# A float32 layer pair: token tiles of both halves in turn ahead of each feed-forward, stores on the ACT queue, another buffer layout in the down phase

## The chip, the cores and the metric

One NeuronCore of a Trainium2 chip. The time is that of one execution in device microseconds, lower is better. Times are medians of several runs; the profile is one further execution.

## What is computed

Two transformer layers one after the other on one sequence of 1024 tokens of width 1024, in float32, with one output of the same shape. The first has a pooling and a differential attention mixer and a gated feed-forward, the second a gated linear attention and a sliding window mixer, cross attention and a convolutional feed-forward. Cut to what the change touches:

```python
# first layer
h = h + rms_norm(jnp.einsum('bsd,de->bse', m, w_out), mix_post_g)
u = rms_norm(h, ffn_pre_g)
f = jax.nn.silu(jnp.einsum('bsd,df->bsf', u, w_ffn_gate)) * jnp.einsum('bsd,df->bsf', u, w_ffn_up)
h = h + rms_norm(jnp.einsum('bsf,fd->bsd', f, w_ffn_down), ffn_post_g)
...
# second layer, last part
h = h + cross_attn(rms_norm_2(h, norm_cross[l]), ...)
h = h + conv_ffn(rms_norm_2(h, norm_ffn[l]), w_up[l], conv_w[l], conv_b[l], w_down[l])
return rms_norm_2(h, norm_final)

def conv_ffn(h, w_up, conv_w, conv_b, w_down):
    u = h @ w_up                       # 1024 x 5632
    u = ...                            # causal convolution of width 3 over the tokens, per channel
    gate, val = jnp.split(u, 2, axis=-1)
    return (jax.nn.silu(gate) * val) @ w_down
```

## The kernel before, in words

Every matmul is done in three: each operand x is split into a high part (`bh`, `wh`: an ACT cast) and a low part (`bl`, `wl`: a DVE subtraction, L54 and L55, function `split`), and hi*hi, lo*hi and hi*lo are summed in PSUM (L75 to L77, L687 to L689). The 1024 tokens are eight tiles of 128; tiles 0 to 3 are the first half and 4 to 7 the second. `big` holds the transposed activations of each half as `bh0/bl0` (`_64`, `_65` in the rows) and `bh1/bl1` (`_66`, `_67`).

**The projection ahead of a feed-forward** (`close_square`, called for `wo`, `wo2` and `woc`) goes through the token tiles in the order 0 to 7. For each tile it multiplies (`mm(i, 0)`, `mm(i, 1)`), and `core` adds the residual (tile `x`, one buffer) and stores the sum to DRAM (`h1d`, `h3d`, `h4d`). `norm_un` squares and sums it on ACT, takes the reciprocal root on POOL and scales it on DVE (L146). Two tiles later `next_T` transposes it on PE: `to_T` (L156) for a tile of the first half; `u_second` (L719) for one of the second half, if a feed-forward follows.

**The feed-forwards** (`ffn`) use a seven-product scheme over 2x2 blocks: token halves by halves of the inner width. `u_second` makes the left forms: a11 and a12 are the first half's blocks, a22, s1, s2, s3 and s4 combine both halves, so tile 4 needs tile 0, 5 needs 1, and so on. In the kernel before it first rebuilds the first half's values r11 and r12 as hi + lo on POOL (L713), and one subtraction (L728) and the split of s3 are POOL's too.

**The up phase** goes over 22 weight tiles: gate weight `wraw` (two raw buffers), up weight `ru` (one). `t_forms` makes the right forms with four POOL sums (L771 to L775), `early` multiplies a11 and a12 by the gate weight, `rest` the other five products; L804 and L805 add up v, then comes the activation. PE takes the early products of three tiles ahead, and the first three before the loop. After each even tile `down_t` makes the right forms of the down weights for that step k (four loads, four POOL adds L821, four stores to `td`); after each odd one `down_s` makes the left forms s1, s2, s4 and a difference on DVE and stores seven blocks to `sd`.

**The down phase** (`down7`) reads both back in blocks of 512 KB into eight raw buffers `r` (L890), splits each and multiplies; the order of products is a11, s1, s2, s4, s3, a22, with six blocks of plain weights (`ws`) before a22 and the eighth operand, a12, at the end. There are 78 such blocks. `final` then normalizes: after the first feed-forward `left` loads h1, stores h2 (`h2d`, L1046) and prepares the next mixer.

A scheduler of the framework sets the order on each engine from the program's order and its own costs. All transfers are issued on the SP queue, in order: one that waits holds all behind it.

## Time and profile before

| | |
|---|---|
| median of 3 runs | 2789.79 us (2788.11 to 2793.65) |
| the profiled execution | 2791.67 us, span 2790.1 us, mean granted clock 0.984 |
| PE / DVE / ACT / POOL busy | 2679.0 / 1663.6 / 1143.4 / 609.7 us |
| first feed-forward, up phase | about 709 to 1167 us |
| first feed-forward, down phase | about 1167 to 1400 us |
| second feed-forward, up phase | about 2096 to 2570 us |
| second feed-forward, down phase | about 2571 us to the end |

PE is TensorE, DVE VectorE, ACT ScalarE, POOL GpSimd, SP the queue that issues transfers. "Idle" in brackets is the engine's idle time just before a group of instructions, with what ended it. Durations of single PE instructions overlap; their starts tell the pace.

### The profile page before, as it was taken

The page shows a single profiled execution, that of the slowest core. Times are in us where ns is not written, and L with a number is a line of the kernel's source. Part 1 is how long each engine was busy: PE and PEld are TensorE (multiplying, and loading weights), DVE is VectorE, ACT ScalarE, POOL GpSimd, SP SyncE. Part 2 cuts the span into 40 slices and gives each one's busy share as a digit, 9 for nine tenths or more (in the row PEclk, how much of TensorE's full clock was granted, in tenths as well). Part 3 has the DMA queues.
Part 4 walks back from the last instruction along what each step waited for, and adds up shares of the span by engine and source line. Part 5 has one row for each costly group of instructions (what it writes and reads, how often), then busy time and mean ns, then how long its engine had stood idle before and what let it go on. Part 6 is the DMA issues. An engine that isn't in the chain of part 4 may idle for free. (4 is left out here: it accounts for less than half of the span.)

```text
span 2790.1 us, 33443 instructions
## 1 busy us (share of the span) xinstructions
PE 2679.0 (96%) x12618; PEld 2179.0 (78%) x12618; DVE 1663.6 (60%) x2536; ACT 1143.4 (41%) x1950; POOL 609.7 (22%) x457
## 2 busy tenths in 40 slices
PE   8999999999699999999899999999997999999998
PEld 7776788888478888788788877888875777777887
DVE  6657415354665555446645557544547999997555
ACT  5555413133333333344443266342324444444443
POOL 1000000001655555000101000000017556652000
PEclk9999999999899999999999999999998999999999
DMA  3000111132344444486321102341223434444863
GB/s 132 31 16 12 53 46 42 56 124 91 106 172 145 148 162 151 176 269 226 123 81 38 57 20 94 133 129 31 70 91 108 159 133 150 155 152 153 295 230 128
DMA packets 145058, 327.04 MB, mean 117 GB/s; under 512 B 13168, under 2 KB 25856, under 8 KB 144896
## 3 DMA queue, kind: packets, MB, share of 16 engines
q1 hardware_dynamic: 144896, 324.91, 34.0%
q8 instruction: 99, 1.62, 0.2%
q14 instruction: 63, 0.52, 0.1%
HBM read 238.87 MB, written 85.98 MB: 116 GB/s over the span
## 5 line engine op out<-in xcount | busy, mean ns | idle before, releaser
L116 POOL TENSOR_TENSOR rstd<-ms,mhalf 128x1 f32<-128x1 f32 (+1 forms) x106 | 63.7, 604 | 1301.7 <-DVE ms L114 878.6
L55 DVE TENSOR_TENSOR wl<-wraw,wh 128x1024 fp32r<-128x1024 f32 (+2 forms) x161 | 201.0, 1253 | 219.9 <-ACT wh L54 215.4
L687 PE MATMUL single<-bh,wh 128*128 128x512 f32 x704 | 280.9, 404 | 42.4 <-ACT wh L54 26.5
L75 PE MATMUL gemm<-bh,wh 128*128 128x512 f32 x800 | 319.7, 400 | 0.0
L77 PE MATMUL gemm<-bh,wl 128*128 128x512 f32 x800 | 317.6, 397 | 0.7 <-DVE wl L55 0.7
L76 PE MATMUL gemm<-bl,wh 128*128 128x512 f32 x800 | 318.2, 398 | 0.0
L54 ACT CAST wh<-wraw 128x1024 fp32r<-128x1024 f32 (+2 forms) x161 | 160.9, 1002 | 302.8 <-PE gemm L76 161.9
L688 PE MATMUL single<-bl,wh 128*128 128x512 f32 x704 | 277.9, 395 | 2.7 <-DVE bl L55 2.7
L689 PE MATMUL single<-bh,wl 128*128 128x512 f32 x704 | 276.6, 393 | 0.0
L687 PEld LDWEIGHTS single<-bh,wh 128*128 128x128 f32 x704 | 134.6, 191 | 85.5 <-DVE v L805 31.4
L55 DVE TENSOR_TENSOR wl<-sum,wh 128x1024 fp32r<-128x1024 f32 x88 | 133.5, 1517 | 94.1 <-ACT wh L54 92.9
L54 ACT CAST wh<-sum 128x1024 fp32r<-128x1024 f32 x88 | 92.7, 1053 | 230.4 <-PE single L688 196.9
L821 POOL TENSOR_TENSOR tmp<-tmp 128x512 f32<-128x512 f32 x88 | 149.0, 1695 | 148.3 <-DMA tmp<-w2d 71.4
L75 PEld LDWEIGHTS gemm<-bh,wh 128*128 128x128 f32 x800 | 151.5, 189 | 33.3 <-issue 3.2
L77 PEld LDWEIGHTS gemm<-bh,wl 128*128 128x128 f32 x800 | 151.5, 189 | 32.7 <-DVE wl L55 1.1
L76 PEld LDWEIGHTS gemm<-bl,wh 128*128 128x128 f32 x800 | 151.5, 189 | 31.9 <-issue 1.1
L688 PEld LDWEIGHTS single<-bl,wh 128*128 128x128 f32 x704 | 134.5, 191 | 30.4 <-DVE bl L55 3.4
L689 PEld LDWEIGHTS single<-bh,wl 128*128 128x128 f32 x704 | 133.8, 190 | 29.5 <-DVE wl L55 0.6
L75 PE MATMUL gemm<-wh,bh 128*128 128x256 f32 (+2 forms) x448 | 151.8, 341 | 1.7 <-ACT wh L54 1.6
L77 PE MATMUL gemm<-wh,bl 128*128 128x256 f32 (+2 forms) x448 | 150.2, 336 | 0.0
L76 PE MATMUL gemm<-wl,bh 128*128 128x256 f32 (+2 forms) x448 | 149.6, 334 | 0.0
L55 DVE TENSOR_TENSOR bh<-r,bh 128x1024 fp32r<-128x1024 f32 x72 | 86.3, 1222 | 86.9 <-ACT bh L54 86.5
(406 smaller groups left out, 6510.7 us busy)
## 6 DMA issues: line engine op xcount, KB each, us to landing
r<-sd SPq DMA_DIRECT2D x60, 512.0 KB, 5.5
td<-tmp SPq DMA_DIRECT2D x88, 256.0 KB, 2.1
r<-td SPq DMA_DIRECT2D x40, 512.0 KB, 6.1
sd<-tmp SPq DMA_DIRECT2D x66, 256.0 KB, 2.3
wraw<-wg SPq DMA_DIRECT2D x22, 512.0 KB, 3.4
ru<-wu SPq DMA_DIRECT2D x22, 512.0 KB, 3.8
tmp<-wd SPq DMA_DIRECT2D x44, 256.0 KB, 3.8
sd<-v SPq DMA_DIRECT2D x44, 256.0 KB, 2.2
```

The source lines that it names most:

```text
L54: nc.scalar.copy(hi, src)
L55: (eng or nc.vector).tensor_tensor(out=lo, in0=src, in1=hi.bitcast(F32), op=ALU.subtract)
L75: nc.tensor.matmul(out, ah, bh, start=(i == 0), stop=False)
L76: nc.tensor.matmul(out, ah, bl, start=False, stop=False)
L77: nc.tensor.matmul(out, al, bh, start=False, stop=(i == n - 1))
L116: nc.gpsimd.tensor_tensor(out=r, in0=ms, in1=self.mhalf[:, 0:w], op=ALU.pow)
L687: nc.tensor.matmul(out, w[0], m[0], start=start, stop=False, skip_group_check=more)
L688: nc.tensor.matmul(out, w[0], m[1], start=False, stop=False, skip_group_check=more)
L689: nc.tensor.matmul(out, w[1], m[0], start=False, stop=stop, skip_group_check=more)
L821: nc.gpsimd.tensor_tensor(out=x, in0=x, in1=y, op=ALU.add)
```

## The change

- `close_square` goes through the tiles as 0, 4, 1, 5, 2, 6, 3, 7 where a feed-forward follows (`wo` and `woc`).
- The first half's transposes are copied once more by ACT (`keep`, tile `raw`), and `u_second` takes r11 and r12 from there. Its subtraction and the split of s3 go from POOL to DVE.
- `up_first` loads and splits three gate weights, the third through a buffer of another tag; `t_forms` loads that third weight a second time for its sums.
- The stores to h1d, h2d, h3d and h4d are issued on the ACT queue, behind the square that reads the same tile; so are the `sd` stores of the last step k.
- The right forms of both down weights are made in the first feed-forward's up phase, those of w2d after its odd tiles; the second one makes none.
- `down7` has two pools of four raw buffers, `ra` first in memory and `rb`. From block 49 on all blocks take `ra`, and `final` takes `rb`.

How the order of instructions changes, at three places. First PE where the first projection ends and the feed-forward begins: `un_6030`, `un_6140` and `un_6225` are tiles 5, 6 and 7 before; `un_6069`, `un_6159` and `un_6252` are tiles 6, 3 and 7 in the change. Before:

```order
L719 MATMUL single_6200<-ident_68,un_6030 128x128 x4
L719 MATMUL single_6205<-ident_68,un_6030 128x128 x4
L719 MATMUL single_6263<-ident_68,un_6140 128x128 x4
L719 MATMUL single_6268<-ident_68,un_6140 128x128 x4
L687 MATMUL single_6288<-bh0_64,wh_6165 128x512
L688 MATMUL single_6288<-bl0_65,wh_6165 128x512
```

In the change:

```order
L723 MATMUL single_6227<-ident_68,un_6069 128x128 x4
L723 MATMUL single_6232<-ident_68,un_6069 128x128 x4
L160 MATMUL single_6285<-ident_68,un_6159 128x128 x4
L160 MATMUL single_6293<-ident_68,un_6159 128x128 x4
L693 MATMUL single_6301<-bh0_64,wh_6184 128x512
L693 MATMUL single_6302<-bh0_64,wh_6184 128x512
```

The early products now stand behind tile 3's transposes, which they read. The hi*hi matmuls of four products go first.

DVE at the same place; `x_6226` (before) and `x_6253` (change) are tile 7's residual, `bl0` the low part of the first half, `bl1` that of the second. Before:

```order
L675 SCALAR_TENSOR_TENSOR un_6225<-single_6169,rstd1_6235,gain_5434 128x512
L677 TENSOR_TENSOR x_6226<-x_6226,un_6225 128x1024
L727 TENSOR_TENSOR t1_6260<-single_6268,r21_6259 128x512
L114 TENSOR_SCALAR ms1_6243<-ss1_6241 128x1
L146 SCALAR_TENSOR_TENSOR un_6225<-x_6226,rstd1_6245,gain_5436 128x1024
L729 SCALAR_TENSOR_TENSOR r11_6257<-t1_6260,r11_6257 128x512
L55 TENSOR_TENSOR bl1_67<-single_6268,bh1_66 128x4x128
L730 SCALAR_TENSOR_TENSOR r12_6258<-r12_6258,r11_6257 128x512
```

In the change:

```order
L732 TENSOR_TENSOR r21_6225<-raw_6142,r21_6225 128x512
L55 TENSOR_TENSOR bl1_67<-single_6232,bh1_66 128x4x128
L733 SCALAR_TENSOR_TENSOR raw_6142<-t1_6226,raw_6142 128x512
L55 TENSOR_TENSOR bl1_67<-t1_6226,bh1_66 128x4x128
L734 SCALAR_TENSOR_TENSOR raw_6142<-raw_6142 128x512
L55 TENSOR_TENSOR s2l_5847<-raw_6142,s2h_5846 128x4x128
L55 TENSOR_TENSOR s3l_5849<-r21_6225,s3h_5848 128x4x128
L55 TENSOR_TENSOR s4l_5851<-raw_6142,s4h_5850 128x4x128
L684 TENSOR_TENSOR x_6253<-x_6253,un_6252 128x1024
L55 TENSOR_TENSOR bl0_65<-single_6285,bh0_64 128x4x128
L55 TENSOR_TENSOR bl0_65<-single_6293,bh0_64 128x4x128
L114 TENSOR_SCALAR ms1_6270<-ss1_6267 128x1
```

Tile 7's residual add stands behind tile 6's forms, and the two splits of tile 3 (`bl0`) behind both.

ACT at the end of the first feed-forward's up phase; `g_9290` and `g_9449` are the last tile's gate, `r` the first blocks of the down phase. Before:

```order
L800 COPY v_9291<-single_9294 128x512
L801 COPY v_9291<-single_9264 128x512
L54 CAST bh0_64<-r_9408 128x1024
L1006 ACTIVATE g_9290<-single_9264 128x512
L54 CAST bh0_64<-r_9412 128x1024
L54 CAST bl0_65<-r_9416 128x1024
```

In the change:

```order
L54 CAST bh1_66<-r_9603 128x1024
L54 CAST bl1_67<-r_9635 128x1024
L1020 ACTIVATE g_9449<-single_9423 128x512
L820 DMA sd_81<-v_9450 128x512 x2
L820 DMA sd_81<-tmp_9524 128x512
L820 DMA sd_81<-tmp_9525 128x512
L820 DMA sd_81<-v_9310 128x512
L820 DMA sd_81<-tmp_9526 128x512
L54 CAST bh0_64<-r_9583 128x1024
L54 CAST bh0_64<-r_9587 128x1024
```

The last silu is followed by six stores, the last of them of `down_s`'s last form, and then by the casts of the first product's blocks.

The diff, cut to its core:

```diff
-    def norm_un(self, h, g, un):
+    def norm_un(self, h, g, un, dst=None):
         nc = self.nc
         ss = self.tiny(1, "ss")
         nc.scalar.activation(un, h, AF.Square, accum_out=ss)
+        if dst is not None:
+            nc.scalar.dma_start(out=dst, in_=h)
         r = self.rstd(ss, D)
         nc.vector.scalar_tensor_tensor(out=un, in0=h, scalar=r, in1=g, op0=ALU.mult, op1=ALU.mult)
 
-    def to_T(self, un, big, i, bank):
+    def to_T(self, un, big, i, bank, keep=False):
         nc = self.nc
         half, c = divmod(i, 4)
+        if keep:
+            self.raw = self.pus.tile([128, KT, 128], F32, tag="raw", name="raw")
         s = slice(c * 128, (c + 1) * 128)
         for k4 in range(2):
             ps = bank()
                 nc.tensor.transpose(ps[:, kt * 128:(kt + 1) * 128], un[:, x:x + 128], self.ident)
             self.split(big["h", half][:, k4 * 4:k4 * 4 + 4, s], big["l", half][:, k4 * 4:k4 * 4 + 4, s],
                        ps.rearrange("p (k t) -> p k t", k=4))
+            if keep:
+                nc.scalar.copy(self.raw[:, k4 * 4:k4 * 4 + 4, :], ps.rearrange("p (k t) -> p k t", k=4))

...
-            self.to_T(un, big, i, bank)
+            self.to_T(un, big, i, bank, self.second is not None)

...
-        self.td = tc.dram_tile([4, NK, 128, 512], F32, name="td")
+        self.td = {w: tc.dram_tile([4, NK, 128, 512], F32, name="td" + w) for w in ('wd', 'w2d')}

...
-            for i in range(2):
+            order = [0, 4, 1, 5, 2, 6, 3, 7] if self.second is not None else list(range(NT))
+            for i in order[:2]:
                 if (i, 0) not in pss:
                     mm(i, 0)
-            for i in range(NT):
+            for n, i in enumerate(order):
                 mm(i, 1)
-                if i >= 2:
+                if n >= 2:
                     self.next_T(self.single)
                 un = self.un()
-                h = core(p, i, (pss[i, 0], pss[i, 1]), un, gs)
-                self.norm_un(h, gs[-1], un)
+                h, dst = core(p, i, (pss[i, 0], pss[i, 1]), un, gs)
+                self.norm_un(h, gs[-1], un, dst)
                 self.pend.append((un, new, i))
-                if i + 2 < NT and (i + 2, 0) not in pss:
-                    mm(i + 2, 0)
-                if extra and extra.get(i):
-                    extra[i]()
+                if n + 2 < NT and (order[n + 2], 0) not in pss:
+                    mm(order[n + 2], 0)
+                if extra and extra.get(n):
+                    extra[n]()

...
-            nc.sync.dma_start(out=self.h1d[i], in_=x)
-            return x
+            return x, self.h1d[i]

...
-        r11, r12, r21, s1 = (self.pus.tile([128, 4, 128], F32, tag=n, name=n) for n in ("r11", "r12", "r21", "t1"))
-        for r, n in ((r11, "a11"), (r12, "a12")):
-            h, l = f[n]
-            nc.gpsimd.tensor_tensor(out=r, in0=h[:, :, s].bitcast(F32), in1=l[:, :, s].bitcast(F32), op=ALU.add)
+        r11, r12 = self.raw[:, 0:4, :], self.raw[:, 4:8, :]
+        r21, s1 = (self.pus.tile([128, 4, 128], F32, tag=n, name=n) for n in ("r21", "t1"))
...
         nc.vector.tensor_tensor(out=s1, in0=ps[1], in1=r21, op=ALU.subtract)
-        nc.gpsimd.tensor_tensor(out=r21, in0=r11, in1=r21, op=ALU.subtract)
+        nc.vector.tensor_tensor(out=r21, in0=r11, in1=r21, op=ALU.subtract)
         nc.vector.scalar_tensor_tensor(out=r11, in0=s1, scalar=-1.0, in1=r11, op0=ALU.mult, op1=ALU.subtract)
         nc.vector.scalar_tensor_tensor(out=r12, in0=r12, scalar=-1.0, in1=r11, op0=ALU.mult, op1=ALU.subtract)
         put("a22", ps[1])
         put("s1", s1)
         put("s2", r11)
         put("s4", r12)
-        put("s3", r21, nc.gpsimd)
+        put("s3", r21)
 
     def up_first(self, wg):
-        self.rg0 = self.up_rg(wg, 0)
+        self.rg0 = [self.up_rg(wg, 0), self.up_rg(wg, NK)]
+        x = self.pw.tile([128, 1024], F32, tag="wl", name="wr", bufs=self.nw)
+        self.nc.sync.dma_start(out=x, in_=self.d[wg][1])
+        self.rg0.append((None, self.up_pair(x)))

...
+                if rg is None:
+                    rg = self.pw.tile([128, 1024], F32, tag="wraw", name="wraw", bufs=self.nraw)
+                    nc.sync.dma_start(out=rg, in_=d[wg][t])
...
-                nc.sync.dma_start(out=self.sd[form, k], in_=x)
-
-            def down_t(k):
-                b = []
-
+                (nc.scalar if k == NK - 1 else nc.sync).dma_start(out=self.sd[form, k], in_=x)
+
+            def down_t(wd, k):
...
-                    nc.sync.dma_start(out=self.td[n, k], in_=x)
+                    nc.sync.dma_start(out=self.td[wd][n, k], in_=x)

...
-            pre = [self.rg0]
+            pre = self.rg0
             self.flush(self.single, 1)
-            ps = [early(pre[0][1])]
-            pre.append(self.up_rg(wg, order[1]))
-            ps.append(early(pre[1][1]))
+            ps = [early(pre[0][1]), early(pre[1][1])]
             w = t_forms(order[0], pre[0][0])
-            pre.append(self.up_rg(wg, order[2]))
             self.flush(self.single)
             ps.append(early(pre[2][1]))
...
                 if n % 2 == 0:
                     fa = x
-                    down_t(n // 2)
+                    if wd == 'wd':
+                        down_t('wd', n // 2)
                 else:
                     down_s(n // 2, fa, x)
+                    if wd == 'wd':
+                        down_t('w2d', n // 2)
...
-        with self.pool("acca") as pa, self.pool("p2") as p2, self.pool("accb") as pb, \
-                self.pool("ws") as pws, self.pool("r4") as pr:
-            acc = [(pa if i < 4 else pb).tile([128, 1024], F32, name=f"acc{i}") for i in range(NT)]
+        with self.pool("ra") as pra, self.pool("p2") as p2, self.pool("rb") as prb, \
+                self.pool("acc") as pa, self.pool("ws") as pws:
+            acc = [pa.tile([128, 1024], F32, name=f"acc{i}") for i in range(NT)]
+            nr = [0]
 
             def r4():
-                return pr.tile([128, 1024], F32, tag="r", name="r", bufs=8)
+                return prb.tile([128, 1024], F32, tag="r", name="r", bufs=4)
 
             def blocks(src, n):
-                t = r4()[:, 0:n * 512]
+                nr[0] += 1
+                if nr[0] <= 4 or nr[0] % 2 or nr[0] > 48:
+                    t = pra.tile([128, 1024], F32, tag="r", name="r", bufs=4)
+                else:
+                    t = r4()
+                t = t[:, 0:n * 512]
                 nc.sync.dma_start(out=t.rearrange("p (k c) -> p k c", k=n), in_=src.rearrange("k p c -> p k c"))
                 return t

...
-                    return self.td[b[1], k:k + n]
+                    return self.td[wd][b[1], k:k + n]
...
-                nc.sync.dma_start(out=net.h2d[i], in_=a)
                 ss = net.tiny(1, "ss")
                 nc.scalar.activation(un, a, AF.Square, accum_out=ss)
+                nc.scalar.dma_start(out=net.h2d[i], in_=a)
...
```

## Rows read from the trace of the kernel before

**Rows 1.** The page's part 1: busy time of each engine, share of the span, instructions.

```profile
PE 2679.0 (96%) x12618; PEld 2179.0 (78%) x12618; DVE 1663.6 (60%) x2536; ACT 1143.4 (41%) x1950; POOL 609.7 (22%) x457
```

**Rows 2.** Busy time by stretch (both up phases, first down phase); columns stand in the row.

```profile
770.00:1120.00 350.00, 349.80 (x1510) 281.28 (x1509) 194.80 (x183) 117.36 (x164) 179.82 (x109) 1.00 0.45 155
1190.00:1340.00 150.00, 150.00 (x663) 124.23 (x662) 83.72 (x83) 72.54 (x94) 0.00 (x0) 1.00 0.72 240
2180.00:2520.00 340.00, 327.92 (x1400) 260.82 (x1401) 311.97 (x236) 155.01 (x185) 204.22 (x102) 1.00 0.44 152
```

**Rows 3.** PE's timeline, start of the first feed-forward: start, duration, group, [idle before <- releaser].

```profile
691.71 1.03 PE L719 MATMUL single<-ident,un 128*128 128x128 f32 x8
...
707.35 1.97 PE L719 MATMUL single<-ident,un 128*128 128x128 f32 x8 [8.24 <-DVE un L146]
...
721.03 1.03 PE L719 MATMUL single<-ident,un 128*128 128x128 f32 x8
738.02 0.80 PE L687 MATMUL single<-bh,wh 128*128 128x512 f32 x1 [15.96 <-ACT wh L54]
...
754.93 0.50 PE L687 MATMUL single<-s4h,vh 128*128 128x512 f32 x1 [3.62 <-ACT v L800]
```

**Rows 4.** PE's timeline, start of the second feed-forward.

```profile
2081.07 1.03 PE L719 MATMUL single<-ident,un 128*128 128x128 f32 x8
...
2120.39 0.80 PE L687 MATMUL single<-bh,wh 128*128 128x512 f32 x1 [10.51 <-ACT wh L54]
...
2130.80 0.56 PE L688 MATMUL single<-bl,wh 128*128 128x512 f32 x1 [2.66 <-DVE bl L55]
...
2137.82 0.39 PE L687 MATMUL single<-s4h,vh 128*128 128x512 f32 x1
```

**Rows 5.** The SP queue's timeline, start of the first feed-forward: issues of transfers.

```profile
733.66 0.33 SPq L742 DMA_DIRECT2D wraw<-wg  x1
```

**Rows 6.** POOL's timeline, start of the first feed-forward.

```profile
724.43 1.65 POOL L713 TENSOR_TENSOR r<-bh,bl 128x512 f32<-128x512 f32 x1 [3.03 <-DVE s2l L55]
```

**Rows 7.** DVE's timeline, start of the first feed-forward.

```profile
700.74 2.28 DVE L677 TENSOR_TENSOR x<-x,un 128x1024 f32<-128x1024 f32 x1
...
720.17 1.77 DVE L729 SCALAR_TENSOR_TENSOR r<-t,r 128x512 f32<-128x512 f32 x1
721.87 0.68 DVE L55 TENSOR_TENSOR bl<-single,bh 128x512 fp32r<-128x512 f32 x1
```

**Rows 8.** PE's waits in 2020:2180 and 2180:2520: us, times, longest.

```profile
PE single L687 <- ACT v L801: 2.8, 1, 2.8
...
PE single L687 <- DVE v L805: 13.8, 16, 2.5
```

**Rows 9.** L805 by form, in 800:1105 and 2195:2530: count, durations, first and last start.

```profile
L805 DVE TENSOR_TENSOR v<-v,single x16: 686/687/689, 810.3 to 1102.3; 128x512 f32<-128x512 f32 x16
...
L805 DVE TENSOR_TENSOR v<-v,single x17: 672/673/675, 2198.8 to 2526.1; 128x512 f32<-128x512 f32 x17
```

**Rows 10.** The page's part 5: the POOL adds of the down weights' forms.

```profile
L821 POOL TENSOR_TENSOR tmp<-tmp 128x512 f32<-128x512 f32 x88 | 149.0, 1695 | 148.3 <-DMA tmp<-w2d 71.4
```

**Rows 11.** Timelines of PE, ACT and DVE at the first feed-forward's hand-over.

```profile
1167.26 1.19 PE L687 MATMUL single<-bh 128*128 128x512 f32 x4 [2.80 <-ACT bh L54]
1169.36 0.79 PE L688 MATMUL single<-bh 128*128 128x512 f32 x1 [0.91 <-DVE bh L55]
...
1166.17 1.03 ACT L54 CAST bh<-r 128x1024 fp32r<-128x1024 f32 x1
...
1169.82 1.22 DVE L55 TENSOR_TENSOR bl<-r,bl 128x1024 fp32r<-128x1024 f32 x1
...
1172.16 0.68 DVE L841 SCALAR_TENSOR_TENSOR tmp<-v,tmp 128x512 f32<-128x512 f32 x1
```

**Rows 12.** Loads of the down phase (L890) in 1190:1320, by form, and their landing.

```profile
L890 SPq DMA_DIRECT2D r<-sd x25: 332/360/1807, 1190.0 to 1315.1; - x25
...
DMA to landing us min/median/max: 2.5/4.9/7.6
```

More of the change, by code (lines that the diff above doesn't have):

```diff
@@ L1543, in core @@
                 nc.vector.tensor_tensor(out=x[:, s], in0=x[:, s], in1=ps[c], op=ALU.add)
-            nc.sync.dma_start(out=self.h3d[i], in_=x)
-            return x
+            return x, self.h3d[i]
         self.close_square(self.sq, 'wo2', 'wo2', ['norm_cross_2'], core, c, ex)
@@ L1709, in core @@
                 nc.vector.tensor_tensor(out=x[:, s], in0=x[:, s], in1=ps[c], op=ALU.add)
-            nc.sync.dma_start(out=self.h4d[i], in_=x)
-            return x
+            return x, self.h4d[i]
         self.close_square(self.sq, 'woc', 'woc', ['norm_ffn_2'], core, u,
```

## The prediction

> **What bounds the kernel now.** I read the busy shares first, then busy time by stretch, then what TensorE waits for in each stretch where it isn't full, then the timelines of the engines behind those waits. PE is busy 2679.0 us of a span of 2790.1 [rows 1], so all that a reordering can win is 111 us of PE idle time plus the slow clock behind each gap. The stretches say where it lies [rows 2]. The first feed-forward's up phase and its down phase are full (349.80 of 350 and 150.00 of 150 us); the second one's up phase is not (327.92 of 340, with DVE at 311.97). The rest sits where a projection ends and a feed-forward starts. In the first, PE idles 8.24 us for the transposes of token tile 6, 15.96 us for the third gate weight and 3.62 us for v [rows 3]; in the second 10.51 and 2.66 us stand out [rows 4]. The reader should see that none of these is a lack of PE work as such: the work behind them waits for one late item.
>
> The 15.96 us are the clearest. The third weight's load can start only when its raw buffer is free, at 733.66 [rows 5]. What frees it is the last of POOL's four sums of the first up tile, and those began late: POOL was still at L713, the rebuilding of r11 and r12, at 724.43, after a wait of 3.03 us for DVE [rows 6].
>
> **The change, part by part.** Times are counted from the end of the projection of the last but one pair (691.71 and 2081.07), where PE's stream is the same in both kernels.
>
> *Start of feed-forward 1.* Before, the product with s4 starts at 754.93, so 63.2 us after it [rows 3]. Removed: the wait for the third weight (three gate weights are now loaded and split ahead, none behind a sum), the L713 adds, and POOL's part in each second-half tile, which DVE takes over (two operations of about 0.68 us, eight more per feed-forward). Added: ACT copies the first-half transposes once more, two operations a tile, beside the projection's matmuls, when ACT is not waited for. New is what comes late next. The early products need tile 3, and that is now the last but one tile: its two splits stand on DVE behind tile 6's nine operations and tile 7's residual add (the DVE order above). Tile 6 is transposed at about +7; nine operations of 0.6 us, tile 7's two gain multiplies (1.4) and its add (2.28 [rows 7], or 1.22, as other operations of its size [rows 11]) put the splits' end at +19, or at +23 if POOL's sums stretch them, as they did the 1.77 us operation [rows 7]. I take +21, between the two. Then 12 us of early products (until 721.03, from 709 [rows 3]), 1 us of transposes, and the 13.3 us that PE worked between 738.02 and the s4 product (16.9 less the wait of 3.62): 47.3 in place of 63.2. **-16 us**; bounds -10 (splits at +27) and -20 (at +17).
>
> *Start of feed-forward 2.* The same sum: 21, 12 and 1, then the 14.8 us between 2120.39 and 2137.82 without the wait of 2.66 [rows 4]: 48.8 in place of 56.75, -8. A wait of 2.8 us for v [rows 8] falls later in the same stretch and hangs on the sums, which can now run some us earlier: -1 of it. **-9 us**; bounds -3 and -15.
>
> *Up phase of feed-forward 2.* It starts its last v addition every 20.46 us (16 intervals in 327.3 us), feed-forward 1 every 19.47 (15 in 292.0) [rows 9], the products being the same; PE's waits for that v come to 13.8 us [rows 8]. The change takes 44 POOL adds of 1695 ns mean [rows 10] out of every even tile. The odd tiles keep their four down forms on DVE, so I give the even ones the whole 0.99 us and the odd ones nothing: 8 x 0.99. **-8 us**; bounds -3 (DVE stays the slower engine in most tiles) and -14 (all of the wait).
>
> *Up phase of feed-forward 1* gets those 44 adds, with 44 loads and 44 stores. DVE has 194.80 us of 350 there, POOL 179.82 [rows 2]; POOL grows by 44 x 1.3 to 1.7, still under 260. Hidden beside PE: **0**. If that cover goes, it is the second rival. The SP queue carries 88 more transfers; its waits for POOL sit ahead of the next tile's loads, two tiles before PE needs them.
>
> *Hand-over to the down phase.* Before, ACT splits the first blocks ahead of the last silu, and PE is back at 1167.26 and fully at 1169.36, after waits of 2.80 and 0.91 us [rows 11]. Now six stores stand on ACT's queue between that silu and the first block's cast, and the last of them waits for the last down form. That form started at 1172.16, behind two block splits like that of 1169.82 (1.15 us from start to start); without these it ends near 1170.6. Cast and split, 1.03 us and 1.22 [rows 11], bring PE back in full at about 1172.6: **+3 us**, and the same for the second feed-forward, **+3 us**. What a store costs ACT to issue no row shows; SP's 0.32 to 0.8 us are the nearest. Bounds -3 each (the 3.7 us of waits go, since weight blocks lie there already) and +6.
>
> *Down phase.* Up to block 48 there are eight raw buffers as before; the last 30 blocks have four. A buffer's turn is issue 0.36, landing 4.9 median and 7.6 at most [rows 12], cast 1.03, split 1.22: 7.5 to 10.2 us, so 1.9 to 2.6 us per block with four. The last two products are 264 matmuls of 0.226 us (150.00 us by 663 [rows 2]), 60 us in which the 30 blocks pass, 2.0 each. PE never waits there now. I take **0** by the median; bounds 0 and +8 each (30 x 0.55, less the 8 us that four full buffers last).
>
> *Stores on ACT.* The next x load waits for the store out of the one x buffer, whichever queue issues it, so nothing in the projections; behind the first feed-forward the w2v loads no longer stand behind h2d stores, but the norm ahead of the mixer is as late as before: **0**, at best some 2 us.
>
> Sum: -16 - 9 - 8 + 0 + 3 + 3 + 0 + 0 = -27 us. Against the profiled execution's 2791.67 us (span 2790.1) that is 2764.7; the median of the runs is 1.9 us below that execution, so 2763 us.
>
> **Rivals.** *The starts give half.* The early products, which in the kernel before had their four tiles long ready, now wait behind a long DVE queue. Should DVE and POOL collide in it all along, the splits come 8 and 5 us later than I take, and the starts give 8 and 4 us: 2776. For: DVE operations beside POOL took 1.7 to 2.3 us in place of 0.68 to 1.22 [rows 7, 11]. Against: POOL loses 16 adds and eight subtractions there.
>
> *Feed-forward 1 takes on feed-forward 2's pace.* The moved adds run in odd tiles, beside the down forms. Adds that hold up DVE operations by 1 us each are what the second feed-forward shows; if 19 intervals grow by 0.99 us, +19: 2782. Against it: DVE is at 56% there, not 92% [rows 2].
> The Trainium skill (SBUF — State Buffer, "SBUF: two separate sides") says that VectorE and GpSimd share a port pair as an exclusive lock, held for the whole instruction, the other blocked: a rule that speaks for this rival, and the stretched operations of rows 7 agree with it. By the rule alone the 44 adds, at the 1.7 us of rows 10, would take 75 us from DVE; it has 155 us idle in that stretch [rows 2], so PE would lose the 19 us only if they fall into the chain that ends with v.
>
> *More than I count.* All of the second up phase's wait goes (-14), the starts reach their better bounds (-20, -15), the hand-overs cost nothing, and the mixer behind starts 0 to 2 us sooner: 2741.
>
> *Four raw buffers starve the down phase: slower.* If each block lands as late as the latest row (7.6 us) and its cast and split queue for another 1.5 us on ACT and DVE, a turn is 11.7 us, 2.9 per block against the 2.0 needed: 30 x 0.9 = 27, less 8 for the full buffers, 19 us in each feed-forward, +38: 2801. It decides from a turn of 8 us on. Against: 7.6 us was seen with up to eight in flight, and the median turn is 7.5.
>
> **How the numbers follow.** A measurement of this kernel tells some 0.2% (5.6 us) from no change. The forecast and its near neighbours, 2749 to 2777, have 0.50, half starts 0.16, the larger gain 0.15, the slower pace 0.08, starving 0.07, and 0.04 that costs eat the gains (2786 to 2796). The first three and most of the fourth are faster: 0.87; same 0.06; slower 0.07. The range 2739 to 2786 takes in the forecast's bounds and three rivals, and leaves out starving, the last case and the tails.
>
> **What would show it.** Right: no wait for the third gate weight; one wait of 8 to 12 us for tile 3's splits in each start, s4 about 47 and 49 us after the projection pair; feed-forward 2 at about 20 us a tile, feed-forward 1 still at 19.47; waits of about 6 us at each hand-over; no PE wait in the down phases. Wrong: feed-forward 1's intervals at 20 or more, PE waiting for casts of r in the last two products, or the starts' gaps merely renamed.

## The result and the profile after

The changed kernel takes 2767.0 us (median of 4 runs, 2765.85 to 2769.0) against 2790.31 us (4 runs), a ratio of 0.9916 with a 95% interval of 0.9899 to 0.9933. Its profiled execution has a span of 2764.1 us, 26.0 below that of before, so the 23.3 us of the medians can be looked for in the traces. TensorE's busy time in the page's part 1 is 7.7 us less at the same count of instructions [rows 1]; POOL has 32 instructions fewer, DVE 16 more.

```profile
PE 2671.3 (97%) x12618; PEld 2175.9 (79%) x12618; DVE 1631.4 (59%) x2552; ACT 1153.4 (42%) x1966; POOL 510.8 (18%) x425
```

FF1 and FF2 are the two feed-forwards, a start is the stretch from a projection's end to a filled up phase, a hand-over the stretch from an up phase to its down phase. I cut both traces at marks that they share: the transposes ahead of the last projection pair (691.71 and 2081.07 before, 690.46 and 2071.45 after), the start of the addition that completes v (DVE) for an early and for the 22nd up tile, the first product of the down phase, the first transposes of what follows. The table has the length of each piece in us; the pieces add up to the 26.0.

| piece | before | after | difference | predicted |
|---|---|---|---|---|
| ahead of the first start | 691.7 | 690.5 | -1.2 | 0 |
| start 1, to the second tile's v | 85.15 | 70.28 | -14.9 | -16 |
| the other 20 up tiles of FF1 | 383.84 | 384.48 | +0.6 | 0 |
| hand-over 1 | 6.56 | 14.45 | **+7.9** | +3 |
| down phase 1 | 192.55 | 191.94 | -0.6 | 0 |
| mixers between | 721.26 | 719.84 | -1.4 | 0 to -2 |
| start 2, to the fifth tile's v | 138.94 | 124.38 | -14.6 | -9 |
| the other 17 up tiles of FF2 | 344.99 | 337.57 | -7.4 | -8 |
| hand-over 2 | 6.64 | 11.66 | **+5.0** | +3 |
| down phase 2 to the end | 218.46 | 219.04 | +0.6 | 0 |

The busy time by stretch of the kernel after, beside [rows 2], shows the three phases in which nothing should be lost: FF1's up phase is full, with POOL at 216.12 in place of 179.82, the down phase is full, in its last stretch with four raw buffers too (1264:1350), and FF2's up phase has 333.62 us of 340 in place of 327.92.

```profile
770.00:1120.00 350.00, 350.00 (x1510) 281.21 (x1509) 199.73 (x183) 115.26 (x161) 216.12 (x141) 1.00 0.61 209
1190.00:1320.00 130.00, 130.00 (x575) 107.72 (x574) 75.06 (x75) 67.79 (x88) 0.00 (x0) 1.00 0.68 224
1264.00:1350.00 86.00, 86.00 (x381) 71.20 (x380) 49.08 (x58) 37.43 (x54) 2.16 (x4) 1.00 0.54 176
2180.00:2520.00 340.00, 333.62 (x1436) 267.93 (x1435) 280.66 (x240) 156.83 (x188) 114.18 (x64) 1.00 0.26 93
```

PE's timeline at the first start (compare [rows 3]) has no wait for a third weight any more. What replaced it are waits of at most 3.69 us; the s4 product starts at 733.50, 43.0 us after the mark in place of 63.2, and then 4.50 us are given back at 744.70, where PE has run ahead of v.

```profile
690.46 1.04 PE L160 MATMUL single<-ident,un 128*128 128x128 f32 x8
...
701.54 0.66 PE L160 MATMUL single<-ident,un 128*128 128x128 f32 x4 [3.69 <-DVE un L148]
703.46 1.11 PE L160 MATMUL single<-ident,un 128*128 128x128 f32 x4 [1.26 <-DVE un L682]
706.39 0.80 PE L693 MATMUL single<-bh,wh 128*128 128x512 f32 x1 [1.81 <-ACT bh L54]
...
710.00 0.79 PE L694 MATMUL single<-bl,wh 128*128 128x512 f32 x1 [0.76 <-DVE bl L55]
...
733.50 0.39 PE L693 MATMUL single<-s4h,vh 128*128 128x512 f32 x1
...
744.70 0.80 PE L693 MATMUL single<-bh,wh 128*128 128x512 f32 x1 [4.50 <-DVE v L815]
```

At the second start (compare [rows 4]) one wait of 7.87 us stands, for tile 3's casts; s4 is at 2117.54, 46.1 us after its mark.

```profile
2087.61 1.71 PE L693 MATMUL single<-bh,wh 128*128 128x512 f32 x3 [7.87 <-ACT bh L54]
2090.95 0.79 PE L694 MATMUL single<-bl,wh 128*128 128x512 f32 x1 [1.63 <-DVE bl L55]
...
2117.54 0.39 PE L693 MATMUL single<-s4h,vh 128*128 128x512 f32 x1
```

PE's waits in 2180:2520 (us, times, longest) are down to 6.4 us in eight tiles, from 13.8 in sixteen [rows 8]:

```profile
PE single L693 <- DVE v L815: 6.4, 8, 0.8
```

### The profile page after: what moved, and what is told of

It reads as the page before. It is cut to its first block, busy times and chain, and to the rows that moved or that the text cites. A ratio compares the mean times of both kernels' runs of the same rounds, so it can differ in the third digit from the quotient of the medians.

```text
span 2764.1 us, 33408 instructions
## 1 busy us (share of the span) xinstructions
PE 2671.3 (97%) x12618; PEld 2175.9 (79%) x12618; DVE 1631.4 (59%) x2552; ACT 1153.4 (42%) x1966; POOL 510.8 (18%) x425
## 4 chain that ended last, share of the span: by engine, by line
PE 62%; DVE 6%; issue 2%; ACT 2%; DMA 1%; POOL 0%; SPq 0%; DVEq 0%; POOLq 0%; ACTq 0%
PE single L693 13%; PE single L694 13%; PE single L695 12%; PE gemm L75 5%; PE gemm L76 5%; PE gemm L77 5%; PE single L75 2%; PE single L76 2%; PE single L77 2%; DVE cv L1740 1%; DVE cv L1742 1%; DVE wl L55 1%; DVE tmp L843 1%; DVE bl L55 1%; PE single L1451 0%
## 5 line engine op out<-in xcount | busy, mean ns | idle before, releaser
L55 DVE TENSOR_TENSOR wl<-sum,wh 128x1024 fp32r<-128x1024 f32 x88 | 114.3, 1299 | 93.5 <-ACT wh L54 91.2
L829 POOL TENSOR_TENSOR tmp<-tmp 128x512 f32<-128x512 f32 x88 | 127.5, 1454 | 97.4 <-DMA tmp<-w2d 45.0
```

The source lines that it names most:

```text
L55: (eng or nc.vector).tensor_tensor(out=lo, in0=src, in1=hi.bitcast(F32), op=ALU.subtract)
L829: nc.gpsimd.tensor_tensor(out=x, in0=x, in1=y, op=ALU.add)
```

## What the kernel loses at a hand-over

The pieces that went wrong are the hand-overs. In the first, ACT's timeline shows the last silu, six stores, and only then the casts of the first product's blocks:

```profile
1147.32 1.05 ACT L54 CAST bl<-r 128x1024 fp32r<-128x1024 f32 x1 [0.23 <-DMA r<-wd]
1149.01 0.60 ACT L1020 ACTIVATE g<-single 128x512 f32<-128x512 f32 x1 [0.64 <-PE single L695]
1150.90 0.89 ACTq L820 DMA_DIRECT2D sd<-v  x2
1151.83 1.25 ACTq L820 DMA_DIRECT2D sd<-tmp  x2
1153.62 0.33 ACTq L820 DMA_DIRECT2D sd<-v  x1
1157.27 0.33 ACTq L820 DMA_DIRECT2D sd<-tmp  x1
1157.63 1.99 ACT L54 CAST bh<-r 128x1024 fp32r<-128x1024 f32 x2 [8.02 <-DMA sd<-v]
```

DVE's last form starts at 1152.90 and takes 0.69, so the sixth store could go at 1153.6. It goes at 1157.27, 3.7 us later, and the idle time before the cast is put down to the landing of an earlier store: the first of the six, issued at 1150.90, landed 6.3 us later. Why the sixth waits for that one no row shows. SP's queue in the same stretch first loads four weight blocks of the first product's later steps (the row has the last three); then comes a load that waits for DVE's split of such a block (1147.12 to 1148.35), and block 1, an `sd` block, behind it (blocks are counted in the program's order, 1 and 2 being the two operands of the first product's first step):

```profile
1142.70 1.45 SPq L904 DMA_DIRECT2D r<-wd  x3
1148.38 0.37 SPq L904 DMA_DIRECT2D r<-tdwd  x1
1148.80 0.46 SPq L904 DMA_DIRECT2D r<-sd  x1
```

PE waits 10.7 us in place of 2.80 [rows 11]:

```profile
1159.67 1.65 PE L693 MATMUL single<-bh 128*128 128x512 f32 x3 [10.70 <-ACT bh L54]
```

Two suspects, then: the stores on ACT, and the pools that set the loads' order. Block 1 landed at 1153.5 and block 2 at 1155.8 (4.7 and 6.5 us after their issues), so of ACT's 8.02 us without work only the last 1.8 found both blocks ready. By that the stores cost some 2 to 3 us here (an estimate), the loads' order the rest.

## Experiments

Pieces in us by the cuts above; ratios are to the kernel before, with 95% intervals.

**order_only**: the kernel before with the new order of tiles alone.

```diff
+            order = [0, 4, 1, 5, 2, 6, 3, 7] if self.second is not None else list(range(NT))
-            for i in range(NT):
+            for n, i in enumerate(order):
```

> The kernel before with the new tile order alone; third gate weight, POOL adds, stores and pools as before. My theory: the larger part of the starts' gain comes from the third gate weight no longer waiting for POOL's sums, so the order alone wins at most what the 8.2 us wait and the tiles' earlier forms give: 3 to 10 us, 2780 to 2787. Rival: the order does nearly all of it (tiles of the second half come earlier, so POOL's adds and sums do too): 20 us or more, below 2771. Third: the order alone costs, since tile 3's splits come last and the third weight still waits: above 2790.

Measured: 2776.55 us, 0.996 [0.9945, 0.9974]. Start 1 is 74.65 (-10.5), start 2 136.97 (-2.0). The order alone does most of the first start and almost nothing of the second. The time lies below the theory's 2780, and the theory is refuted where it matters: with the third gate weight still loaded behind the first tile's sums, PE's 15.96 us for the third weight [rows 3] are down to 3.1 (waits in 690:780), because the second half's tiles come earlier and POOL's first sum starts at 714.97, 25.2 us after the mark, in place of 34.3:

```profile
PE single L688 <- ACT wh L54: 3.1, 1, 3.1
```

**starts_only**: order, raw copies, POOL's part of each tile on DVE, and three gate weights; the stores, the moved adds and the pools as before (diff against the changed kernel, cut).

```diff
-            nc.scalar.dma_start(out=dst, in_=h)
...
-                (nc.scalar if k == NK - 1 else nc.sync).dma_start(out=self.sd[form, k], in_=x)
+                nc.sync.dma_start(out=self.sd[form, k], in_=x)
...
-                    if wd == 'wd':
-                        down_t('wd', n // 2)
+                    down_t(n // 2)
```

> The kernel before with everything that changes at the two starts (tile order, raw copies in place of the POOL adds, POOL's part on DVE, three gate weights ahead), and nothing else. By the two traces the starts gain 15 and 10 to 15 us, and nothing here touches the hand-overs or the second up phase's pace: -25 to -29, so 2761 to 2765, which is below the whole change's 2767. Rival: the start of the second feed-forward owes 4 us of its gain to the POOL adds that left its first tiles: then -20 to -22, 2768 to 2770.

Measured: 2769.98 us, 0.9935 [0.992, 0.9949]; starts 72.87 and 129.27, -12.3 and -9.7. That is 1.8 and 7.7 us beyond the order's share, and 2.6 and 4.9 us short of the whole change. So the time is the rival's (2768 to 2770), not the 2761 to 2765 that I expected, and edits that I had put at nothing in the starts belong to them.

**move_forms**: the kernel before with the adds of w2d moved into FF1, nothing else.

```diff
-                    down_t(n // 2)
+                    if wd == 'wd':
+                        down_t('wd', n // 2)
...
+                    if wd == 'wd':
+                        down_t('w2d', n // 2)
```

> The kernel before with the right forms of w2d made in the first up phase, and nothing else. My theory: the second up phase falls to alternating 19.45 and 20.45 us a tile, 8 us, the first stays at 19.47: -7 to -10, 2780 to 2783. Rival 1: the first up phase takes part of it back (its DVE busy beside POOL): -2 to +5, 2788 to 2795. Rival 2: the start of the second gains as well, since three adds fall together with its first sums: -11 to -14, 2776 to 2779.

Measured: 2783.03 us (10 runs), 0.9985 [0.9975, 0.9994]. FF2's up phase is 337.60, the -7.4 of the whole change; start 2 is 2.2 shorter. FF1's up phase is 386.02, 2.2 longer in this trace, and the end 2.3 longer, in an execution 3 us above its median. FF1's piece lies between 384.4 and 386.2 in all variants, with the moved adds or without, so the 2.2 us there are not theirs. That the whole gives 4.8 us and not 9.5, and not the 7 to 10 that I expected, is not accounted for.

**old_pools**: the whole change, with `down7`'s pools as before.

```diff
-        with self.pool("ra") as pra, self.pool("p2") as p2, self.pool("rb") as prb, \
-                self.pool("acc") as pa, self.pool("ws") as pws:
+        with self.pool("acca") as pa, self.pool("p2") as p2, self.pool("accb") as pb, \
+                self.pool("ws") as pws, self.pool("r4") as pr:
...
-                return prb.tile([128, 1024], F32, tag="r", name="r", bufs=4)
+                return pr.tile([128, 1024], F32, tag="r", name="r", bufs=8)
```

> The whole change with the down phase's pools as before (one pool of eight raw buffers, last in memory), stores of the last step still on ACT. The whole change loses 7.3 and 5.6 us at the two hand-overs. Theory A: the loss is the load of the first block, which stands on the SP queue behind a load that waits for the split of an early weight block; with one pool the blocks come in order and PE is back some 4 to 6 us sooner at each: 2756 to 2760. Theory B: the loss is the six stores on ACT's queue in front of the first cast, pools play no part: 2765 to 2769. Theory C: the early blocks need memory at its start, and without it everything is later: above 2770.

Measured: 2754.25 us, 0.9877 [0.9862, 0.9892], 12.8 us faster than the whole change (10.3 when each is counted from the kernel before as it ran beside it). Hand-overs 6.52 and 6.64, as before; all other pieces within 1.4 us of the whole change's, down phase 1 with eight buffers 192.52 against 191.94 with four. SP's and ACT's timelines show why. Block 1 and five more are loaded in order, and the stores stand on ACT behind three casts:

```profile
1144.77 0.38 SPq L898 DMA_DIRECT2D r<-sd  x1
```

```profile
1148.78 1.04 ACT L54 CAST bh<-r 128x1024 fp32r<-128x1024 f32 x1 [9.01 <-DMA r<-sd]
1149.72 0.59 ACT L1014 ACTIVATE g<-single 128x512 f32<-128x512 f32 x1
1150.21 1.03 ACT L54 CAST bh<-r 128x1024 fp32r<-128x1024 f32 x1
1151.30 1.05 ACT L54 CAST bl<-r 128x1024 fp32r<-128x1024 f32 x1
1152.24 0.81 ACTq L820 DMA_DIRECT2D sd<-v  x2
```

**old_handover**: old pools, and the last step's stores on SP too (the `put` line of the next diff).

> The whole change with pools as before and all stores of the last step on SP, to be read beside the run with the old pools alone (2754.25 us, hand-overs of 6.5 and 6.6 us, as in the kernel before). If the stores on ACT neither cost nor give anything once the casts stand ahead of them: 2752 to 2756, same hand-overs. If SP, freed of them, had carried the down phase's loads sooner: 2757 or more. If they still cost ACT time there: below 2752.

Measured: 2754.26 us, 0.9878 [0.9864, 0.9893]; hand-overs 6.48 and 6.64. With one pool the queue of these stores makes no difference.

**sp_stores**: the whole change, only the last step's stores back on SP.

```diff
-                (nc.scalar if k == NK - 1 else nc.sync).dma_start(out=self.sd[form, k], in_=x)
+                nc.sync.dma_start(out=self.sd[form, k], in_=x)
```

> The whole change, but the last step's seven stores are back on the SP queue; the pools stay. Theory B (ACT's stores made the hand-overs slow): the first cast follows its load at once, 4 to 6 us less at the first hand-over, 2 to 3 at the second: 2757 to 2761. Theory A (SP's order and the pools): nothing won, and SP's loads of blocks 2 to 4 now stand behind the stores: 2766 to 2774.

Measured: 2769.71 us, 0.9931 [0.9917, 0.9946]; hand-over 1 is 18.56, longer still. Block 1 is cast at 1151.06, but the next block's load now stands on SP behind six stores and four loads, at 1155.47, and PE starts at 1161.48 after 14.80 us:

```profile
1148.59 0.81 SPq L820 DMA_DIRECT2D sd<-v  x2
...
1152.49 2.93 SPq L825 DMA_DIRECT2D tmp<-w2d  x4
1155.47 0.43 SPq L904 DMA_DIRECT2D r<-wd  x1
```

**rb_late**: the whole change, with the first eight blocks in `ra`, which takes the wait for a split from ahead of block 1's load.

```diff
-                if nr[0] <= 4 or nr[0] % 2 or nr[0] > 48:
+                if nr[0] <= 8 or nr[0] % 2 or nr[0] > 48:
```

> The whole change, but blocks 6 and 8 of the down phase take the first pool too, so that the load of block 1 no longer stands on SP behind a load that waits for the split of block 6; the six stores still stand on ACT in front of the first cast. Theory A (SP's order made the hand-overs slow): they fall from 14.5 and 11.7 us to about 7 to 9: 2755 to 2760. Theory B (ACT's stores did, with a store that waited some 3.6 us for an earlier store's end): the first stays at 13 to 15, 2765 to 2769.

Measured: 2764.18 us, 0.9909 [0.9892, 0.9925]; hand-overs 13.15 and 10.43. Block 1 is loaded at 1145.38, yet its cast stands behind the stores as before:

```profile
1157.17 0.33 ACTq L820 DMA_DIRECT2D sd<-tmp  x1
1157.54 1.99 ACT L54 CAST bh<-r 128x1024 fp32r<-128x1024 f32 x2 [6.71 <-DMA sd<-tmp]
```

**rb_late_sp**: the edits of sp_stores and rb_late together.

> The whole change with its two pools of raw blocks, but with both cures of the hand-over at once: the wait of the second pool's first blocks is put off (as in rb_late), and the stores of the last step stay on SP (as in sp_stores). Theory, that the hand-over is long because either queue has stores ahead of the first down blocks: the first casts stand on ACT right behind the silu and their loads ahead of the stores on SP, so the wait of PE for the first block's halves falls from 7.87 to 10.7 us to about 3, and only the blocks loaded behind the six stores can still be late, so the hand-over of FF1 takes 7 to 10 us (13.2 and 18.6 with one cure alone) and the kernel 2756 to 2762 us. Rival, that the place of the raw blocks in memory is itself what slows their loads or splits: the hand-over stays at 13 us or more, the kernel at 2764 to 2770 us.

Measured: 2768.9 us, 0.9924 [0.9908, 0.9941]. Hand-over 1 is 8.68, inside the theory's 7 to 10 and well below the rival's 13; PE's first wait is 4.92 where the theory had 3. But the time of the kernel missed the theory, since the wait came again some 14 us later and made down phase 1 8.5 to 9.6 us longer (201.05) than in the other two-pool kernels. PE's timeline shows the second wait:

```profile
1154.94 1.22 PE L693 MATMUL single<-bh 128*128 128x512 f32 x2 [4.92 <-ACT bh L54]
...
1168.66 1.22 PE L693 MATMUL single<-bl 128*128 128x512 f32 x2 [4.50 <-ACT bl L54]
```

The cast it waited for needs a `wd` block that SP issued at 1163.65, behind the stores and loads of the last step:

```profile
1151.94 0.81 SPq L820 DMA_DIRECT2D sd<-v  x2
...
1155.33 2.77 SPq L825 DMA_DIRECT2D tmp<-w2d  x4
...
1161.91 1.70 SPq L830 DMA_DIRECT2D tdw2d<-tmp  x2
1163.65 0.44 SPq L904 DMA_DIRECT2D r<-wd  x1
```

Of the 9 us, 4.50 and 0.93 (1170.81) are waits; the granted clock in the row of 1169:1177 (its third number from the end) accounts for 8 x 0.35 = 2.8 us more:

```profile
1169.00:1177.00 8.00, 7.08 (x21) 5.14 (x21) 5.10 (x5) 3.91 (x5) 0.67 (x1) 0.65 0.96 322
1177.00:1190.00 13.00, 13.00 (x60) 10.74 (x59) 6.66 (x7) 5.79 (x7) 0.00 (x0) 1.00 0.93 320
```

So at hand-over 1 it is the order on both queues. Hand-over 2 (10.44 here) is another matter: in the whole change the first product's hi casts go at 2542.07 and 2543.98, ahead of the stores on ACT (from 2545.54), and still it stayed above 10 in all four two-pool kernels, 6.64 with one pool. The whole change's waits of SP in 2515:2540 name it. The queue stood 20.8 us for a matmul of the up phase; then it loaded four weight blocks, waited 2.3 us for a split, and loaded block 1 only at 2536.88, 2.7 us after the last wait for v (2534.14).

```profile
SPq L904 <- PE single L694: 20.8, 1, 20.8
```

```profile
2530.39 1.93 SPq L904 DMA_DIRECT2D r<-w2d  x4
2536.47 0.37 SPq L904 DMA_DIRECT2D r<-tdw2d  x1
2536.88 0.46 SPq L904 DMA_DIRECT2D r<-sd  x1
```

With one pool (old_pools) block 1 goes first, 6.4 us ahead of that wait (2526.65):

```profile
2520.30 0.37 SPq L898 DMA_DIRECT2D r<-sd  x1
```

In rb_late, without the wait for the split, block 1 goes at 2531.76, and the hand-over is still 10.43; what remains there is the 20.8 us for the matmul and the four loads ahead of block 1.

Which tile's memory that matmul held, no row shows; that `ra`, first in memory, comes free later there is argued, not shown.

**h_on_sp_oldpools**: old pools, with the stores to h1d, h3d and h4d on SP again.

```diff
         if dst is not None:
-            nc.scalar.dma_start(out=dst, in_=h)
+            nc.sync.dma_start(out=dst, in_=h)
```

> The whole change with the old pools, and with the stores of h1d, h3d and h4d back on the SP queue. My prediction put their move at nothing, since the x buffer is free only when the store has landed: 2753 to 2756. The stages of the runs say otherwise: both starts of the whole change are 2.6 and 4.9 us shorter than those of the run that changes the starts alone. If that is the stores (the next loads and the up weights' load stand behind a store that waits on SP), the starts lengthen by 2 to 5 us each: 2758 to 2763.

Measured: 2761.96 us, 0.990 [0.9885, 0.9914], 7.7 us slower than old_pools, and than old_handover, which ran beside it; starts 72.78 and 127.90, +2.6 and +2.8, so 5.4 of the 7.7 lie in the starts. With starts_only this closes the sum of start 1 (10.5 + 1.8 + 2.6 = 14.9). Start 2 comes to 2.0 + 7.7 + 2.2 of the moved adds + 2.8 = 14.7, measured 14.6; but kernels that agree in all four parts have it between 124.0 and 125.7 us, so its terms hold to about 1 us each, where start 1 is 70.2 to 70.4 in all of them. SP's timeline names the mechanism: the load of the up weight (`ru`) waits behind a store of h1 at 709.51:

```profile
709.51 0.33 SPq L146 DMA_DIRECT2D h1d<-x  x1
709.89 9.16 SPq L775 DMA_DIRECT2D ru<-wu  x2
```

With the store on ACT, in the whole change (its mark lies at the same time), it goes 8 us sooner, and POOL's sums begin at 711.38 in place of 714.45:

```profile
701.93 15.01 SPq L775 DMA_DIRECT2D ru<-wu  x2
```

**tile3_early**: old pools, tiles in the order 0, 4, 1, 5, 2, 3, 6, 7, since PE waits for tile 3; POOL rebuilds the values that tile 7 needs.

```diff
-            order = [0, 4, 1, 5, 2, 6, 3, 7] if self.second is not None else list(range(NT))
+            order = [0, 4, 1, 5, 2, 3, 6, 7] if self.second is not None else list(range(NT))
...
+        if i == 7:
+            ...
+                nc.gpsimd.tensor_tensor(out=self.raw[:, k4:k4 + 4, :], in0=h[:, :, s].bitcast(F32), in1=l[:, :, s].bitcast(F32), op=ALU.add)
```

> The whole change with the old pools, and the tiles in the order 0, 4, 1, 5, 2, 3, 6, 7; tile 7's r11 and r12 are rebuilt on POOL, since there is room for one raw copy only. Theory: what is left of the starts' waits is tile 3's splits (some 8 us in the first start, 9.5 in the second), which now come one tile sooner; the early products then wait for tile 6's transposes alone: 3 to 5 us less in each start, 2744 to 2749 against the old pools' 2754. Rival: tile 6's and tile 7's forms become the last item, and the two POOL adds stand in front of the up weights' sums: no gain or a loss, 2753 to 2760.

Measured: 2756.71 us, 0.9886 [0.9869, 0.9902]; no gain, as the rival had it. The starts are 71.18 and 126.53, 1.0 and 1.5 longer than with old_pools: POOL's rebuild stands ahead of its weight sums, which begin at 718.42, 26.3 us after the mark in place of 20.9, and in the first start waits for a weight (3.3 us) and for v (3.2) stand where one of 4.5 for v was.

```profile
715.01 3.46 POOL L720 TENSOR_TENSOR raw<-bh,bl 128x512 f32<-128x512 f32 x2 [3.87 <-DVE s4l L55]
718.42 1.28 POOL L786 TENSOR_TENSOR sum<-wraw,ru 128x512 f32<-128x512 f32 x1
```

**old_pools_again**: the best version a second time, beside tile3_early.

> The whole change with the old pools once more, beside the other run of this call on the same chip: 2752 to 2757.

Measured: 2755.46 us, 0.9877 [0.9863, 0.9892]. So the whole change without its last part, the two pools, beats both kernels.

## Why the prediction was right, and where it was not

The time (2763 against 2767.0, inside 2739 to 2786) and the sign came out, by parts that are not all right and that in part cancel.

- *Start 1*, -16, measured -14.9: the third weight's wait went, but mostly not for the reason given. I credited the three weights loaded ahead; order_only shows that the order of tiles took 12.9 of its 15.96 us, and all that starts_only adds to it is worth 1.8. Tile 3's two splits (DVE, from 709.27, 1.28 us) end 20.1 us after the mark, where I took 21; that is near by luck. The terms that I wrote come to 16 or 17, not to the 19 stated, and tile 6's nine operations began 11.6 us after the mark (702.07), behind the scaling for tile 3, not at 7. s4 came at 43.0 where I had 47.3, since the high halves' products run ahead of those splits (from 706.39); the 4.50 us wait for v took that back: that addition stands on DVE behind a split of POOL's sums (741.15), the next late item, which I had not priced. And no wait of 8 to 12 us for tile 3's splits came in this start, only in the second (7.87).
- *Start 2*, -9, measured -14.6: this term was too small by 5.6 us. Up to s4 it gained 10.7 (46.1 in place of 56.75, where I had 48.8), and 3.9 more by the fifth tile's v. The share of the order is 2.0, of copies, DVE's part and weights 7.7; the rest are the moved adds (2.2) and the stores (2.8).
- *Stores on ACT*, "0 ... nothing in the projections": this step failed. It looked at the x load alone, which waits for the store on either queue. Behind the store on SP stands also the first up weight's load: 2.6 and 2.8 us.
- *FF2's up phase*, -8, measured -7.4: right, by its own mechanism, since the moved adds alone (move_forms) give the same 7.4. The waits for v remain in eight tiles, every other one.
- *FF1's up phase*, 0, measured +0.6, PE full: right, and with it the rival of the slower pace is refuted. POOL grew by 36.3 us in 350 and DVE by 4.9, beside a PE that never waited.
- *Hand-overs*, +3 and +3, bound +6: measured +7.9 and +5.0. I named the stores ahead of the cast, but took the last store as issued when its form ends; it came 3.7 us later. And I took the blocks to lie there already, while the two pools changed the order of their loads. In hand-over 2 the loads' order and the wait for a matmul do it, ahead of any store. The sum itself was 0.25 us short as well: 1170.6, 1.03 and 1.22 make 1172.85.
- *Down phase*, 0 by the median turn: right. PE waits nowhere from 1169 to 1352, nor from 2546 to the end, with eight buffers or with four, so the rival of starving is refuted. The two rivals that halve or double the gains did not come; half starts would be 12 us, they were 29.5.

So the nearness of the total is partly luck: the errors cancel, 4.5 us more from the starts against 6.9 us more lost at the hand-overs.

## What to carry to other kernels

On an in-order queue, ask of every transfer what stands behind it, not only who waits for it: the stores moved off SP gained 5.4 us in the starts through a weight load that nobody had connected with them, and the same kind of move put six stores ahead of the casts that PE needed. A change of buffer pools is also a change of the order in which loads are issued; look where the first block that the next phase needs stands, on the loading queue and on the engine that casts it. Undo a change part by part: here one part, the two pools, gave back 10 to 13 us of the 33.6 that the rest had gained.

## What the runs showed of the hardware that I had not expected

An engine that issues transfers does not compute while one of them waits: ACT stood 3.7 us for a sixth store whose data were complete, and casts whose blocks lay ready stood behind it (in rb_late block 1 landed at 1153.0 and was cast at 1157.54). In both kernels the sixth store went just when the first of the six had landed (1150.90 + 6.3, and 1152.12 + 5.0); in old_pools, with casts between the stores, it went at 1156.92, before the first had landed (1152.24 + 6.0). The issue itself took 0.33 us for a single store on ACT.

Loads issued close together land late: the six of old_pools, 512 KB each, landed 4.0, 4.8, 5.6, 6.4, 7.2 and 7.7 us after their issues. Where block 1 was the fifth of six loads issued in 2.9 us (rb_late_sp, from 1143.27), ACT waited for it until 1152.51, 7.3 us after its issue; with old_pools, as the first of six, it was cast 4.0 us after its issue (1144.77 to 1148.78). So the order in which loads are issued counts as much as their start.

And a gap costs more than its length: behind the second wait of rb_late_sp (4.50 us) the granted clock was 0.65 over 8 us: matmuls start every 0.43 us until about 1174.4 and every 0.23 us after, its two levels of 1.2 and 2.4 GHz, and the next stretch has 1.00.
